# An encoder of two layers on one core: the opening and the last sums rearranged

## The chip, the core and the metric

The kernel runs on one core of one Trainium2 chip. The metric is the device time of one execution in microseconds (us). A core has a matrix engine (TensorE, PE in the profile; its weight loads are shown apart, as PEld), three engines for work on vectors (VectorE, or DVE; ScalarE, or ACT; GpSimd, or POOL), and an engine that here only issues transfers (SyncE, or SP). Each engine works through its own queue in order. Transfers (DMA) are issued by SP, ScalarE and POOL, each into queues of its own, and are carried out by 16 shared transfer engines.

## The reference

Two layers work on x, 512 tokens by 1024 columns of float32. Each does

```
h = rms_norm(x) ;  z = h @ w_in            # q, k, v of two attentions, two gates
ya = window_gqa(q_a, k_a, v_a, sink) @ w_proj_a
yb = neighbourhood_attn(q_b, k_b, v_b, rel_bias) @ w_proj_b
x = x + (sigmoid(g_a) * ya + sigmoid(g_b) * yb) @ w_out
h = rms_norm(x)
x = x + (silu(h @ w_gate) * (h @ w_up)) @ w_down
```

The first attention has 8 query heads, rotary angles made from the positions, and one "sink" value for each head that joins the sum of its softmax. The hidden width of the last line (the FFN) is 2816.

## The kernel before

**Products.** Each float32 matrix is split into a high part (rounded to fp32r, TensorE's fast type for float32) and a low part (the rest), and a product is made of three: high by high, high by low, low by high. One such triple on 512 columns is a *unit*, 0.68 us in the plan (`UNIT`, line 424). Activations mostly lie turned: x is held as eight buffers `xT[k]` (line 746), 128 of the 1024 columns on the partitions and the 512 tokens along the free axis. In them the tokens stand in a permuted order (`by_columns`, `held`, lines 87 to 93).

**The plan.** All weights are cut into slabs of up to four blocks of 128 rows, listed in the order of their use (`slab`, `plan_pair`, `plan_token`, `plan_ffn`, lines 450 to 511). For each slab a time is written down in units of the plan: 23 us ahead of its use `w_load` (line 546) has POOL load the high part, 15 us ahead `w_low` (line 555) has ScalarE write the negated high part into a second buffer, to which POOL's next transfer adds the raw weights. `tick` (line 437) is called after each unit and emits what has come due; so the place of these steps in the engines' queues is set by the count of units done, not by what the chip does. `w_take` hands the slabs out in the plan's order.

**The chains.** Everything beside the stream of products (norms, attention heads, rotary tables) is written as generators, "chains", which say before each step what they need (`Need`, line 358). A first, dry pass keeps a modelled clock for each engine and steps a chain where its needs are met in the model (`drive`, line 413); a string that the main stream yields makes it step the chains until the named work is done. The dry pass also packs all buffers into two arenas. In the profile all of this work has line 310, the helper that emits each instruction; so groups are told apart by operation, shape and tile: `mm` and `at` are the two pools of four PSUM banks each, `arena` all packed buffers, `cst` the constants with the identity matrix for transposes.

**The opening** (lines 697 to 784, 1174 to 1192). POOL fills three small tiles. SP loads the identity and then x in eight chunks of 128 columns; ScalarE's queue loads the norm gains (`vec`) and the first two blocks of the first weight slab; POOL's queue loads the positions, the head gains, the next three slabs (`first_load`), `gqa`, the sink values `snk`, the other constants, and then what the plan asks for, first of all the slabs for K and V. TensorE's first instruction turns the gains. Then the first token product runs (`token_matmul`, line 881, with `begin`): it goes through the eight chunks k in order, with 4 blocks of tokens, 4 units, in each. After the first unit of chunk k it emits `start` for chunk k + 1: four transposes of the chunk, the high and low part of the chunk's weights (`first_parts`: a cast on ScalarE, a subtraction on VectorE), the scaled high part of x, the copy into `xT`, the low part of x, the square, and the running sum of squares. In `start` for chunk 0 the weights' parts come after the scaled copy, for the others before it. The chain `chain_tables` (line 751) makes the rotary tables meanwhile: it needs the positions, the sink values and `gqa`, writes the positions into `vec2`, negates the sink values into `nsnk`, turns `vec2`, and computes cosine and sine in some twenty small steps on VectorE and two Sin steps on ScalarE.

**The end of the FFN** (lines 480 to 511, 1583 to 1685). The hidden columns past the first 256 are made in five quads of 512 by a scheme of seven products of 256 columns (`m_step`); between them `d` steps add the earlier hidden columns, times `w_down`, to x. The last group, four blocks of 128 hidden columns, has its `d` steps at the very end, after all `m` steps. There the `w_down` block is the stationary operand and the 512 tokens move, so the sum has the model's columns on the partitions. For each of the eight blocks c of 128 columns, 12 products are made; in the last layer `evac_d` adds x into a buffer t, and one block later `turn_out` (line 1466) makes four transposes of t, a copy out of PSUM (VectorE and ScalarE in turn) and one write of 256 KB to the output by SP, in pieces of 512 bytes.

In each layer the two projections (4 x 48 products) and `w_out` (4 x 48 products) follow the attention's last head; the gate products, which the stream has ahead of them, don't need it.

Of the kernel before, what the change touches and what calls it, by code (L numbers as in the profile page):

```python
# [86 lines left out]
def by_columns(ap):  # L87

    return ap.rearrange("p (r cc c) -> p cc r c", r=8, c=8)


def held(ap):
    return ap.rearrange("p (cc r c) -> p cc r c", r=8, c=8)
# [116 lines left out]
def trunk(ctx: ExitStack, tc: tile.TileContext, a: dict, out: bass.AP, lay: Layout):  # L210
# [34 lines left out]
    def act(dtype=F32):  # L245
        return buf([S], dtype)

    def mm_bank():
        return pm.tile([P, S], F32, tag="mm", name=nm("mm"))

    def at_bank():
        return pa.tile([P, S], F32, tag="at", name=nm("at"))
# [197 lines left out]
    def slab(n, width, src, units, later_h=0.0, later_l=0.0, on_engines=False):  # L450
        i = len(plan)
        plan.append((n, width, src))
        if on_engines:
            at_pos(total[0] - LEAD_R, lambda: w_raw(i))
            at_pos(total[0] - LEAD_P, lambda: w_parts(i))
        else:
            at_pos(total[0] - LEAD_H + later_h, lambda: w_load(i))
            at_pos(total[0] - LEAD_L + later_l, lambda: w_low(i))
        total[0] += units * UNIT
# [20 lines left out]
    def ffn_steps():  # L480
        groups = [(0, 2)] + [(2 + 4 * i, 4) for i in range(QUADS)]
        steps = []
        for q in range(QUADS):
            ms = [("m", q, w, m) for w in ("w_gate", "w_up") for m in ORDER]
            ds = [("d", *groups[q], c) for c in range(KD)]
            for i, m in enumerate(ms):
                steps.append(m)
                if ds and i >= (1 if q else 5):
                    steps.append(ds.pop(0))
        return steps + [("d", *groups[-1], c) for c in range(KD)]  # L490
# [3 lines left out]
    def plan_ffn(l):  # L494
        plan_pair(a["w_gate"][l], 0, KD, on_engines=True)
        plan_pair(a["w_up"][l], 0, KD)
        for step in ffn_steps():
            if step[0] == "m":
                _, q, w, m = step
                if m == ORDER[0]:  # L500
                    t = total[0]
                    early = 18.0 if q == 0 and w == "w_gate" else 0.0
                    quads[l, q, w] = Quad(a[w][l], 256 + 512 * q, t - early, early > 0.0)
                quads[l, q, w].due(m, total[0] - early)
                early = max(0.0, early - 1.2)
                total[0] += 24 * 0.12
            else:
                _, f0, n, c = step
                if c % 2 == 0:
                    slab(n, 256, [(0, a["w_down"][l][P * f0 : P * (f0 + n), P * c : P * c + 256])], 0, 3.0 if f0 else -7.0, 2.0)  # L510
                total[0] += n * UNIT

    highs, lows, raws, used = {}, {}, {}, [0]

# [26 lines left out]
    def first_parts(k):  # L541
        raw, h, lo = raws[k // 2][:, k % 2], highs[k // 2][:, k % 2], lows[k // 2][:, k % 2]
        A.copy(h, raw)
        V.tensor_tensor(lo, raw, h.bitcast(F32), ALU.subtract)
# [22 lines left out]
    def w_take():  # L567

        i = used[0]
        used[0] += 1  # L570
        w_load(i)
        w_low(i)
        return [(highs[i][:, k], lows[i][:, k]) for k in range(plan[i][0])]
# [120 lines left out]
    vec2T = cp.tile([P, P], F32, tag="vec2T", name="vec2T")  # L694
    ones = cp.tile([P, 2], F32, tag="ones", name="ones")
    magic = cp.tile([P, 32], I32, tag="magic", name="magic")
    G.memset(vec2, 0.0)
    G.memset(ones, 1.0)
    G.memset(magic, 0x5F3759DF)
# [35 lines left out]
    GQ.dma_start(cst[:, P:], a["consts"][:, P:])  # L735
    warm = cp.tile([P, 2], F32, tag="warm", name="warm")
    A.copy(warm, ones)
    ps = at_bank()
    T.transpose(ps[:, :32], vec, ident[:32, :32])
    V.tensor_copy(vecT, ps[:, :32])  # L740
# [5 lines left out]
    xT = [buf([S]) for _ in range(KD)]  # L746
    nsnk = cp.tile([P, DEPTH, 8], F32, tag="nsnk", name="nsnk")
    gb = cp.tile([P, DEPTH], F32, tag="gb", name="gb")
    trig = cp.tile([P, 2, NB, 32], F32, tag="trig", name="trig")

    def chain_tables():
        yield Need("dve", [posi, snk, gqa])
        V.tensor_copy(vec2[64:68], posi[64:68])
        V.tensor_scalar(nsnk, snk, -1.0, None, ALU.mult)
        yield Need("pe", [vec2], [at_slots])
        at_slots.take()
        ps = at_bank()
        T.transpose(ps[:, :P], vec2, ident)
        yield Need("dve", [ps])
        V.tensor_copy(vec2T, ps[:, :P])  # L760
        at_slots.give(clock["dve"])
        posf = vec2T[:, 64:68]
        V.scalar_tensor_tensor(gb, vec2T[:, 0:2], HD ** -0.5, vec2T[:, 2:4], ALU.mult, ALU.mult)
        v3 = lambda t: t[:, : NB * 32].rearrange("p (b f) -> p b f", b=NB)
        ang = v3(act())
        for b in range(NB):
            V.tensor_scalar(ang[:, b, :], cst[:, C_INV : C_INV + 32], posf[:, b : b + 1], None, ALU.mult)
        yield Need()
        for i, shift in enumerate((0.25, 0.0)):
            n, r = v3(act()), v3(act())  # L770
            V.tensor_scalar(n, ang, INV_2PI, shift, ALU.mult, ALU.add)
            V.tensor_scalar(n, n, ROUND_MAGIC, None, ALU.add)
            V.tensor_scalar(n, n, -ROUND_MAGIC, None, ALU.add)
            yield Need()
            V.scalar_tensor_tensor(r, n, -TWO_PI_1, ang, ALU.mult, ALU.add)
            V.scalar_tensor_tensor(r, n, -TWO_PI_2, r, ALU.mult, ALU.add)
            V.scalar_tensor_tensor(r, n, -TWO_PI_3, r, ALU.mult, ALU.add)
            yield Need()
            if shift:
                V.tensor_scalar(r, r, HALF_PI, None, ALU.add)  # L780
            V.tensor_scalar(r, r, PI_LO, -PI_LO, ALU.min, ALU.max)
            A.activation(trig[:, i], r, AF.Sin)
            yield Need()
        done.add("trig")


# [386 lines left out]

    def start(nrm, k):

        ps = at_bank()
        for b in range(NB):
            T.transpose(ps[:, P * b : P * b + P], xin[k][:, b, :], ident)
        if k:
            first_parts(k)  # L1180
        A.activation(held(nrm.xh[k]), by_columns(ps), AF.Copy, scale=gain(0, k))
        if not k:
            first_parts(k)
        A.copy(held(xT[k]), by_columns(ps))
        V.scalar_tensor_tensor(nrm.xl[k], xT[k], gain(0, k), nrm.xh[k].bitcast(F32), ALU.mult, ALU.subtract)
        sq = act()
        A.activation(sq, xT[k], AF.Square)
        if nrm.acc is not None:
            V.tensor_tensor(sq, sq, nrm.acc, ALU.add)
        nrm.acc = sq  # L1190
        if k == KD - 1:
            done.add("acc0")

    def layer(l):
# [266 lines left out]
        last = l == DEPTH - 1  # L1461
        A.activation(warm, ones, AF.Silu)
        spawn(nrm.chain())
        tail = []

        def turn_out():
            k, t = tail.pop(0)
            pt = at_bank()
            for b in range(NB):
                T.transpose(pt[:, P * b : P * b + P], t[:, P * b : P * b + P], ident)  # L1470
            o = act()
            (A.copy if k % 2 else V.tensor_copy)(o, pt)
            Q.dma_start(
                out.rearrange("o (b p) d -> p (o b) d", p=P)[:, :, P * k : P * k + P],
                o.rearrange("p (b n) -> p b n", b=NB),
            )


        xs = {}
# [158 lines left out]
        def add_x(k, o):  # L1638
            V.tensor_tensor(xT[k], xT[k], o, ALU.add)

        def evac_d(k, o):
            if not last:
                add_x(k, o)
                if k % 2:
                    norms[2 * l + 2].chunk(k - 1)
                    norms[2 * l + 2].chunk(k)
                return
            if tail:
                turn_out()
            t = act()  # L1650
            V.tensor_tensor(by_columns(t), held(xT[k]), held(o), ALU.add)
            tail.append((k, t))

        steps_ = ffn_steps()
        for i, step in enumerate(steps_[:-KD]):
            if step[0] == "m":
# [5 lines left out]
            else:  # L1662
# [6 lines left out]
                o = mm_bank()  # L1669
                yield from d_products(o, c, range(f0, f0 + n), wk, True, True)  # L1670
                soon(lambda c=c, o=o: add_x(c, o))
        if not last:
            norms[2 * l + 2] = Norm(2 * l + 2)
        _, f0, n, _ = steps_[-1]
        for c in range(0, KD, 2):
            wk = w_take()
            os_ = [mm_bank(), mm_bank()]
            for half in range(2):
                for j in range(2):
                    fs = range(f0 + 2 * half, f0 + 2 * half + 2)  # L1680
                    yield from d_products(os_[j], c + j, fs, wk[2 * half : 2 * half + 2], half == 0, half == 1)
                    if half:
                        evac_d(c + j, os_[j])
        if tail:
            turn_out()

    def main():
        norms[0] = Norm(0)
# [32 lines left out]
```

## Time and profile before

| | |
|---|---|
| median of 3 runs | 1386.06 us (1385.47 to 1386.4) |
| the profiled execution | 1385.97 us |
| its span, first to last instruction | 1384.2 us |
| TensorE busy | 1370.9 us, 99% |
| VectorE busy | 910.6 us, 66% |
| ScalarE busy | 707.6 us, 51% |
| GpSimd busy | 317.8 us, 23% |
| read from HBM | 193.51 MB |
| transfer engines, 0 to 40 us | 0.84 busy, 203 GB/s |
| TensorE busy, 0 to 40 us | 33.27 us |

How to read it. A row of the timeline gives the start in us from the span's beginning, the length, the engine, the operation, what it writes and reads (out<-in), the shape, and how many instructions are merged in it; in brackets stand the engine's idle time just before and what ended it. The length of a row of several products runs from the first one's start to the last one's end. A single product's length includes the time in which the next one already runs, so the pace is read from rows of many. A row of the stretches view gives a stretch, its length, and for PE, PEld, DVE, ACT and POOL the busy time with the count of instructions; then the clock granted to TensorE, the mean busy share of the transfer engines (it can pass 1 where several queues overlap) and GB/s. A row of the transfers view gives the tile, the issuing queue, the count, the size and the time from issue to landing.

### The profile page before, as it was taken

How to read it: one execution, taken by the hardware profiler on the slowest of the kernel's cores; microseconds unless marked ns; L12 is line 12 of the kernel's file. 1: busy time of each engine (PE TensorE's matmuls, PEld its weight loads, DVE VectorE, ACT ScalarE, POOL GpSimd, SP SyncE). 2: the span in 40 equal slices, each digit the busy share in tenths (PEclk: the TensorE clock that was granted, in tenths of full speed). 3: DMA queues.
4: the chain of work that ended last, by engine and by line, in shares of the span. 5: the costliest groups of instructions: out<-in, count | busy, mean ns of one | idle time of the engine just before them, and what ended most of it. 6: DMA issues, size and time to landing. Idle time of an engine off the chain costs nothing.

```text
span 1384.2 us, 20905 instructions
## 1 busy us (share of the span) xinstructions
PE 1370.9 (99%) x8042; PEld 1211.4 (88%) x8042; DVE 910.6 (66%) x1702; ACT 707.6 (51%) x1171; POOL 317.8 (23%) x326
## 2 busy tenths in 40 slices
PE   8999999999999999999999999999999999999998
PEld 6888888888899999999888888888889999999996
DVE  5875878555976657575648667784568757575663
ACT  6476767634643333343545675785356434343441
POOL 4542222310211110111353422223012111111110
PEclk9999999999999999999999999999999999999999
DMA  8998888874766483735899979879559483645645
GB/s 212 182 173 141 162 156 152 174 174 124 152 151 152 108 197 91 184 93 106 160 188 190 167 138 161 155 139 213 148 117 188 92 213 92 153 122 122 149 84 119
DMA packets 197332, 207.46 MB, mean 150 GB/s; under 512 B 25568, under 2 KB 167056, under 8 KB 197232
## 3 DMA queue, kind: packets, MB, share of 16 engines
q0 software_dynamic: 134976, 141.54, 54.8%
q1 hardware_dynamic: 61904, 64.04, 15.9%
q8 instruction: 63, 1.03, 0.3%
q10 hardware_dynamic: 352, 0.54, 0.1%
q14 instruction: 37, 0.30, 0.1%
HBM read 193.51 MB, written 2.10 MB: 141 GB/s over the span
## 4 chain that ended last, share of the span: by engine, by line
PE 94%; ACT 2%; DMA 1%; DVE 1%; issue 1%; POOL 0%; POOLq 0%; ACTq 0%
PE mm L310 73%; PE at L310 21%; ACT arena L310 2%; DVE arena L310 1%; DMA snk<-in_sink_a 0%; DMA vec<-in_q_norm_b 0%; DMA arena<-in_w_in 0%; ACT L310 0%; POOL posi L310 0%; POOL arena L310 0%; POOL vec L310 0%; ACT trig L310 0%; ACT sm L310 0%; DVE sm L310 0%; DVE den L310 0%
## 5 line engine op out<-in xcount | busy, mean ns | idle before, releaser
L310 PE MATMUL mm<-arena 128*128 128x512 f32 (+1 forms) x5568 | 1113.4, 355 | 2.2 <-ACT arena L310 1.3
L310 PEld LDWEIGHTS mm<-arena 128*128 128x128 f32 x5568 | 905.1, 190 | 137.2 <-DVE arena L310 3.7
L310 ACT CAST arena<-arena 128x1024 fp32r<-128x1024 f32 (+2 forms) x278 | 235.4, 869 | 221.9 <-DVE arena L310 215.8
L310 DVE TENSOR_TENSOR arena<-arena,arena 128x1024 fp32r<-128x1024 f32 (+2 forms) x268 | 262.1, 993 | 49.0 <-ACT arena L310 48.1
L310 PE MATMUL at<-arena 128*128 128x256 f32 (+1 forms) x1952 | 282.8, 289 | 0.4 <-DVE negm L310 0.4
L310 ACT ACTIVATE arena<-arena 128x1024 fp32r<-128x1024 f32 (+3 forms) x252 | 206.6, 843 | 137.7 <-DMA arena<-in_w_down 59.6
L310 PEld LDWEIGHTS at<-arena 128*128 128x128 f32 x1952 | 259.9, 191 | 13.6 <-DVE negm L310 1.4
L310 DVE TENSOR_TENSOR arena<-arena,mm 128x512 f32<-128x512 f32 x144 | 98.8, 686 | 241.8 <-PE mm L310 240.3
L310 POOL DMA_DIRECT2D arena<-in_w_in x163 | 162.6, 1376 | 302.9 <-ACT arena L310 272.7
L310 POOL DMA_DIRECT2D arena<-in_w_down x96 | 99.9, 1241 | 503.1 <-ACT arena L310 347.8
L310 DVE TENSOR_TENSOR arena<-arena 128x1024 f32<-128x1024 f32 (+4 forms) x196 | 158.0, 823 | 2.4
L310 DVE TENSOR_TENSOR arena<-at,arena 128x512 fp32r<-128x512 f32 (+4 forms) x158 | 104.2, 660 | 30.6 <-ACT arena L310 24.1
L310 ACT CAST arena<-at 128x512 fp32r<-128x512 f32 (+2 forms) x116 | 64.4, 555 | 63.3 <-PE at L310 62.0
L310 PE MATMUL at<-cst,arena 128*128 128x128 f32 x472 | 73.9, 276 | 1.9 <-issue 1.4
L310 ACT ACTIVATE arena<-arena,negm 128x256 f32<-128x256 f32 (+1 forms) x128 | 68.2, 534 | 14.5 <-DVE negm L310 12.5
L310 ACT COPY arena<-at 128x512 f32<-128x512 f32 (+1 forms) x68 | 39.6, 582 | 67.0 <-PE at L310 66.5
L310 PEld LDWEIGHTS at<-cst,arena 128*128 128x128 f32 x472 | 58.1, 141 | 11.9 <-issue 1.8
L310 DVE TENSOR_TENSOR arena<-mm,arena 128x512 f32<-128x512 f32 x72 | 49.1, 686 | 25.3 <-PE mm L310 25.1
L310 DVE CUSTOM_DVE_ANT_0 arena<-at,cst,nsnk 128x256 f32<-128x256 f32 (+1 forms) x64 | 34.4, 547 | 34.9 <-PE at L310 34.1
L310 ACT ACTIVATE arena<-arena,vecT 128x512 fp32r<-128x512 f32 x24 | 17.4, 726 | 54.5 <-DVE arena L310 54.1
L310 DVE CUSTOM_DVE_ANT_0 arena<-at,arena 128x256 f32<-128x256 f32 x64 | 26.3, 420 | 17.3 <-PE at L310 17.0
L310 POOL DMA_DIRECT2D arena<-in_w_up x8 | 8.2, 1030 | 126.5 <-PE mm L310 78.8
(68 smaller groups left out, 422.8 us busy)
## 6 DMA issues: line engine op xcount, KB each, us to landing
arena<-in_w_in POOLq DMA_DIRECT2D x99, 512.0 KB, 7.3
arena<-in_w_down POOLq DMA_DIRECT2D x80, 512.0 KB, 6.7
arena<-in_w_gate SPq DMA_DIRECT2D x20, 1024.0 KB
arena<-in_w_up SPq DMA_DIRECT2D x20, 1024.0 KB
arena<-in_w_in POOLq DMA_DIRECT2D x64, 256.0 KB, 6.3
arena<-in_w_proj_a POOLq DMA_DIRECT2D x16, 512.0 KB, 7.3
arena<-in_w_proj_b POOLq DMA_DIRECT2D x16, 512.0 KB, 7.4
arena<-in_w_out SPq DMA_DIRECT2D x16, 512.0 KB
```

The lines of the kernel that those rows point to most:

```text
L310: f(*args, **kw)
```

## The change

In the opening:

- POOL fills one more tile with zeros (`idle`, the first half of `trig`, which gets its tables later), ahead of the other fills. Seven products of this tile with itself, float32, 128 by 128 by 128, are put ahead of TensorE's first transposes, and three more after the transposes of chunk 0 (`turn_over`). Nobody reads their results.
- In `start` the parts of the weights now come before the scaled copy of x for chunk 0 too, and `start` notes that it was emitted (`x0`, `x1`, ...).
- `chain_tables` waits for the positions and for `x2` at its beginning, and no longer for the sink values and `gqa`; these are waited for at its end, where `nsnk` is now made.

At the end of the last layer:

- The last group's slabs are four of 2 x 128 rows by 512 columns, instead of four of 4 x 128 rows by 256 columns.
- The last group's `d` steps are replaced by `finish`: 128 tokens of the hidden block are the stationary operand and 512 columns of `w_down` move, so the sum has the tokens on the partitions. For each half of the columns and each pair of hidden blocks it goes through the four blocks b of tokens, 6 products each.
- x is turned beforehand by the new chain `chain_out` into four buffers `xo[b]`: eight times four transposes and a copy by ScalarE. It may start when the adds of the group before are emitted (`x_out`), which is during the last `w_up` quad; `finish` begins when all of it is emitted (`xo`).
- The sum is added to `xo[b]` in place, and each half row block is written by two transfers of 128 KB, one on SP's queue and one on ScalarE's, in pieces of 2 KB.

```diff
     def plan_ffn(l):
...
+        steps = ffn_steps()
+        for step in steps if l < DEPTH - 1 else steps[:-KD]:
...
+        if l == DEPTH - 1:
+            f0 = steps[-1][1]
+            for half, pair in np.ndindex(2, 2):
+                rows = a["w_down"][l][P * (f0 + 2 * pair) : P * (f0 + 2 * pair + 2)]
+                slab(2, S, [(0, rows[:, S * half : S * half + S])], 0, 3.0, 2.0)
+                total[0] += 2 * NB * UNIT
...
+    trig = cp.tile([P, 2, NB, 32], F32, tag="trig", name="trig")
+    idle = trig[:, 0].rearrange("p b f -> p (b f)")
+
+    def turn_over(n):
+
+        ps = mm_bank()
+        for _ in range(n):
+            T.matmul(ps[:, :P], idle, idle, start=True, stop=True)
+
+    G.memset(idle, 0.0)
     G.memset(vec2, 0.0)
...
     A.copy(warm, ones)
+    turn_over(7)
     ps = at_bank()
     T.transpose(ps[:, :32], vec, ident[:32, :32])
...
     def chain_tables():
-        yield Need("dve", [posi, snk, gqa])
+        yield Need("dve", [posi], keys=["x2"])
         V.tensor_copy(vec2[64:68], posi[64:68])
-        V.tensor_scalar(nsnk, snk, -1.0, None, ALU.mult)
         yield Need("pe", [vec2], [at_slots])
...
             A.activation(trig[:, i], r, AF.Sin)
             yield Need()
+        yield Need("dve", [snk, gqa])
+        V.tensor_scalar(nsnk, snk, -1.0, None, ALU.mult)
         done.add("trig")
...
     def start(nrm, k):
 
+        done.add(f"x{k}")
         ps = at_bank()
         for b in range(NB):
             T.transpose(ps[:, P * b : P * b + P], xin[k][:, b, :], ident)
-        if k:
-            first_parts(k)
+        if not k:
+            turn_over(3)
+        first_parts(k)
         A.activation(held(nrm.xh[k]), by_columns(ps), AF.Copy, scale=gain(0, k))
-        if not k:
-            first_parts(k)
         A.copy(held(xT[k]), by_columns(ps))
...
-        def turn_out():
...
+        def chain_out():
+
+            yield Need(keys=["x_out"])
             for b in range(NB):
-                T.transpose(pt[:, P * b : P * b + P], t[:, P * b : P * b + P], ident)
...
+                xo.append(buf([D]))
+                for half in range(2):
+                    part = xT[4 * half : 4 * half + 4]
+                    yield Need("pe", part, [at_slots])
+                    at_slots.take()
+                    ps = at_bank()
+                    for i in range(4):
+                        T.transpose(ps[:, P * i : P * i + P], part[i][:, P * b : P * b + P], ident)
+                    yield Need("act", [ps])
+                    A.copy(xo[b][:, S * half : S * half + S], ps)
+                    at_slots.give(clock["act"])
+            done.add("xo")
...
+        def finish(f0):
+
+            yield "xo"
+            rows = out.rearrange("o (r cc c) d -> cc (o r) c d", r=8, c=8)
+            for half in range(2):
+                cols = slice(S * half, S * half + S)
+                ps = [mm_bank() for _ in range(NB)]
+                for pair in range(2):
+                    wk = w_take()
+                    for b in range(NB):
+                        t = slice(P * b, P * b + P)
+                        for k, (hi, lo) in enumerate(wk):
+                            h, lw = u[f0 + 2 * pair + k]
+                            mm(ps[b], h[:, t], hi, pair == k == 0, False)
+                            mm(ps[b], h[:, t], lo, False, False)
+                            mm(ps[b], lw[:, t], hi, False, pair == k == 1)
+                            tick(UNIT)
+                            yield UNIT
+                        if pair:
+                            o = xo[b][:, cols]
+                            V.tensor_tensor(o, o, ps[b], ALU.add)
+                            for i, queue in enumerate((Q, AQ)):
+                                queue.dma_start(rows[2 * b + i][:, :, cols], o[64 * i : 64 * i + 64])
```

More of the change, by code (lines that the diff above doesn't have):

```diff
@@ L496, in plan_ffn @@
         plan_pair(a["w_up"][l], 0, KD)
-        for step in ffn_steps():
+        steps = ffn_steps()
+        for step in steps if l < DEPTH - 1 else steps[:-KD]:
             if step[0] == "m":
@@ L748, in trunk @@
     gb = cp.tile([P, DEPTH], F32, tag="gb", name="gb")
-    trig = cp.tile([P, 2, NB, 32], F32, tag="trig", name="trig")
     def chain_tables():
-        yield Need("dve", [posi, snk, gqa])
+        yield Need("dve", [posi], keys=["x2"])
         V.tensor_copy(vec2[64:68], posi[64:68])
-        V.tensor_scalar(nsnk, snk, -1.0, None, ALU.mult)
         yield Need("pe", [vec2], [at_slots])
@@ L1463, in layer @@
         spawn(nrm.chain())
-        tail = []
-        def turn_out():
-            k, t = tail.pop(0)
-            pt = at_bank()
+        xo = []
+        def chain_out():
+            yield Need(keys=["x_out"])
             for b in range(NB):
-                T.transpose(pt[:, P * b : P * b + P], t[:, P * b : P * b + P], ident)
[L1471 to L1476, printed above, removed]
+                xo.append(buf([D]))
[10 more added lines that the diff above has]
+            done.add("xo")
         xs = {}
@@ L1641, in evac_d @@
         def evac_d(k, o):
[L1642 to L1652, printed above, removed]
+            add_x(k, o)
+            if k % 2:
+                norms[2 * l + 2].chunk(k - 1)
+                norms[2 * l + 2].chunk(k)
+        def finish(f0):
[20 more added lines that the diff above has]
+                                queue.dma_start(rows[2 * b + i][:, :, cols], o[64 * i : 64 * i + 64])
+        if last:
+            spawn(chain_out())
         steps_ = ffn_steps()
@@ L1671, in layer @@
                 soon(lambda c=c, o=o: add_x(c, o))
-        if not last:
-            norms[2 * l + 2] = Norm(2 * l + 2)
+                if last and c == KD - 1 and f0 + n == steps_[-1][1]:
+                    soon(lambda: done.add("x_out"))
         _, f0, n, _ = steps_[-1]
+        if last:
+            yield from finish(f0)
+            return
+        norms[2 * l + 2] = Norm(2 * l + 2)
         for c in range(0, KD, 2):
@@ L1683, in layer @@
                         evac_d(c + j, os_[j])
-        if tail:
-            turn_out()
     def main():
```

## The prediction

> **What bounds the kernel now.** I read the page first: shares of the engines, then the chain that ended last.
>
> ```profile
> PE 1370.9 (99%) x8042; PEld 1211.4 (88%) x8042; DVE 910.6 (66%) x1702; ACT 707.6 (51%) x1171; POOL 317.8 (23%) x326
> PE 94%; ACT 2%; DMA 1%; DVE 1%; issue 1%; POOL 0%; POOLq 0%; ACTq 0%
> ```
>
> TensorE is the bound, 99% busy. The change takes no real product away (96 products of 512 columns make the last sums before and after, and 32 transposes turn the result in both), so it can win only where TensorE is slow or stands: in the first 40 us, and after its last product. These are two sums, made below against the profiled execution: 1385.97 us with a span of 1384.2 us, 0.09 us under the median of the runs, 1386.06 us.
>
> For the opening I read the timeline of TensorE; its columns are start and length.
>
> ```profile
> 4.74 1.11 PE L310 MATMUL at<-cst,arena 128*128 128x128 f32 x4 [0.19 <-DMA arena<-in_x]
> 7.14 2.18 PE L310 MATMUL mm<-arena 128*128 128x512 f32 x3 [1.28 <-ACT arena L310]
> 9.83 3.76 PE L310 MATMUL mm<-arena 128*128 128x512 f32 x8
> 18.72 0.60 PE L310 MATMUL at<-cst,arena 128*128 128x128 f32 x4
> 19.08 3.00 PE L310 MATMUL mm<-arena 128*128 128x512 f32 x12
> 21.91 0.60 PE L310 MATMUL at<-cst,arena 128*128 128x128 f32 x4
> 25.21 0.60 PE L310 MATMUL at<-cst,arena 128*128 128x128 f32 x4
> 28.92 0.60 PE L310 MATMUL at<-cst,arena 128*128 128x128 f32 x4
> 32.43 0.60 PE L310 MATMUL at<-cst,arena 128*128 128x128 f32 x4
> 36.33 0.35 PE L310 MATMUL at<-ones,arena 128*128 128x1 f32 x2 [0.31 <-DVE arena L310]
> ```
>
> Eight products from 9.83 take 0.47 us each, twelve from 19.08 take 0.25 us: TensorE runs at half pace at first. The groups of four transposes mark the chunks of x. At full pace one chunk (12 products and 4 transposes) takes 21.91 - 18.72 = 3.19 us; the next ones take 3.30, 3.70 and 3.51 us, and 3.90 us pass from the last transposes to the sums of squares (36.33). Over 3.19 us each these four hold 1.65 us of waiting.
>
> **The sink wait.** The timeline of VectorE, and what TensorE waited for:
>
> ```profile
> 16.89 0.17 DVE L310 TENSOR_SCALAR nsnk<-snk 128x16 f32<-128x16 f32 x1 [3.80 <-DMA snk<-in_sink_a]
> 16.84 0.63 PE L310 MATMUL mm<-arena 128*128 128x512 f32 x2
> 17.71 0.50 PE L310 MATMUL mm<-arena 128*128 128x512 f32 x1 [0.24 <-DVE arena L310]
> 18.38 0.51 PE L310 MATMUL mm<-arena 128*128 128x512 f32 x1 [0.16 <-DVE arena L310]
> ```
>
> VectorE stands 3.80 us for the sink values, with the low half of the third chunk's weights queued behind. TensorE starts the third chunk's first product at 17.07 (the second of the pair from 16.84), the next two at 17.71 and 18.38; at 0.25 us apart they would start at 17.32 and 17.57. The wait costs 18.38 - 17.57 = 0.8 us by itself. Moved to the end of the tables the step finds the values there (they came at 16.89), and nobody waits for it before the first attention scores.
>
> **The products of zeros.** Seven stand ahead of everything on TensorE and need one more fill on POOL.
>
> ```profile
> 0.74 0.21 POOL L310 MEMSET vec<- 128x128 f32 x1 [0.29 <-POOLq L1707]
> 5.89 0.69 ACT L310 ACTIVATE arena<-at,vecT 128x512 fp32r<-128x512 f32 x1 [1.63 <-PE at L310]
> 6.48 0.61 ACT L310 CAST arena<-arena 128x512 fp32r<-128x512 f32 x1
> ```
>
> The fill is of the size of this one, 0.21 us, and puts POOL's early transfer issues off by as much. No row shows a product of zeros; the nearest are the four cold transposes of the same shape (1.11 us in all, 0.28 each) and the cold products of 512 columns (0.47). Seven take 2.0 to 3.3 us. I take 0.47, to be safe. From the fill's end at about 1.0 they run to 4.3; TensorE is free until 4.74, so they hide. The three after the first transposes (0.8 to 1.4 us from 5.85) end by 7.3, about where the first product starts (7.14). ScalarE's first two steps change places: the first product needs both, so it moves by at most 6.48 - 5.89 = 0.6 us, the case that the weights land only at 6.48.
>
> The second chunk's transposes stay at about 9.0 (four cold ones ahead of 9.83), since the three products before them are paced by ScalarE and VectorE. If the clock is up by then, at 3.19 us a chunk the fourth's come at 15.4 instead of 18.72: 3.3 us gained, sink wait included. I do not book this, because of what ScalarE meets next.
>
> ```profile
> 20.55 1.58 ACT L310 ACTIVATE arena<-arena 128x512 f32<-128x512 f32 x2
> 21.09 1.04 ACT L310 ACTIVATE arena<-arena 128x1024 fp32r<-128x1024 f32 x1
> 22.04 0.60 ACT L310 CAST arena<-arena 128x512 fp32r<-128x512 f32 x1
> 24.40 1.28 ACT L310 ACT_TABLE_LOAD   x1
> 12.52 0.54 POOL L310 DMA_DIRECT2D cst<-in_consts  x1 [1.92 <-DMA arena<-in_w_in]
> 13.05 1.52 POOL L310 DMA_DIRECT2D arena<-in_w_in  x2
> arena<-in_w_in POOLq DMA_DIRECT2D x1, 512.0 KB, 7.4
> 16.00:20.00 4.00, 3.60 (x17) 2.46 (x16) 3.08 (x11) 2.02 (x5) 0.00 (x0) 1.00 1.42 339
> ```
>
> The 128x1024 step at 21.09 is `w_low` of the fifth slab, the first of the K and V weights. Its place in ScalarE's queue is fixed by the plan, which counts units: the four slabs ahead hold 32 units of 0.68 us, it is due 15.0 us before their end, so in the tenth unit, right after the fourth chunk's square (20.55). It reads the slab's load, which POOL issued at 13.05 behind a 1.92 us wait on an earlier load and which took 7.4 us: it landed at 20.45. The change touches neither that queue nor its bytes, and the transfer engines were full up to 20 us (share 1.42, the last row). With the fourth chunk at 15.4, ScalarE comes to this step at 15.4 + (21.09 - 18.72) = 17.8 and stands until 20.45, and the fifth chunk's weights and transposes, behind it on ScalarE, stand too. So the 3.3 us shrink to 21.09 - 20.45 = 0.6 us. After that the same chain follows: 0.95 us to the next cast, and the table load of 1.28 us for the sine, now a chunk later because the tables wait for `x2`. There it meets the sixth slab's `w_low` in the same chunk, which can take the 0.6 us away; or the 1.65 us of waiting seen above goes. Bounds 0 and 2.3 us. I take 0.8, near the lower end, since the table work is moved and not reduced.
>
> Tables that end one chunk later (3.2 us) are covered further on:
>
> ```profile
> 258.82 95.23 PE mm L310 x420
> ```
>
> After the last product of the attention TensorE has 420 products in a row, of which the projections take 384; the 36 left are gate products that did not need the attention, 8.2 us of cover.
>
> **The last sums.** The timeline of the end:
>
> ```profile
> 1375.79 1.64 PE L310 MATMUL mm<-arena 128*128 128x512 f32 x6
> 1377.90 0.69 DVE L310 COPY arena<-at 128x512 f32<-128x512 f32 x1 [1.58 <-PE at L310]
> 1378.51 0.68 DVE L310 TENSOR_TENSOR arena<-arena,mm 128x512 f32<-128x512 f32 x1
> 1379.29 0.63 PE L310 MATMUL at<-cst,arena 128*128 128x128 f32 x4 [1.43 <-issue]
> 1379.95 0.59 ACT L310 COPY arena<-at 128x512 f32<-128x512 f32 x1 [2.97 <-PE at L310]
> 1380.56 0.37 SPq L310 DMA_DIRECT2D out<-arena  x1
> 1377.43 0.44 PE at L310 x4
> ```
>
> The last product ends at 1377.43; then come the seventh transposes, a copy, the add, the eighth transposes, a copy, and the last write's issue at 1380.56: 3.13 us. After, one add (0.69 with 0.07 of hops) leads to the issue: 0.76 us. That saves 2.37 us. From issue to the span's end, 3.64 us, I change nothing: it is 256 KB still, on two queues (SP's, and ScalarE's, which has nothing left) in pieces of 2 KB instead of one queue with 512 bytes. I allow 0.3 us either way.
>
> What is given back: the eighth group of transposes now lies in the stream of products, 0.44 us. And the groups come in one burst in the last `w_up` quad, where a rotation of four banks has one in use; ScalarE's copy (0.59 us) is longer than a group (0.44 us), so late groups wait for their bank: over eight of them 0 to 1.2 us, I take 0.4, as three banks carry the first three groups free. ScalarE has the room:
>
> ```profile
> 1341.37 2.00 ACT L310 CAST arena<-arena 128x1024 fp32r<-128x1024 f32 x2 [3.25 <-DVE arena L310]
> ```
>
> It idles 3.25 us there. Without that room the copies would push the casts for the last quad, and the cost would go to the 1.2 us. The slabs stay four of 512 KB, at the same spacing. So the end saves 2.37 - 0.44 - 0.4 = 1.5 us, between 0.4 and 2.2.
>
> Sum: 0.8 + 1.5 = 2.3 us, 1385.97 - 2.3 = 1383.7 us.
>
> **The rivals.** *The opening pays in full.* If the slab lands by 17.8, or the chunks catch up, the opening gives 2.3 to 3.3 us: 1381.2 to 1382.2 us. For it: the half pace and the sink wait are plain in the rows. Against: the 7.4 us load.
>
> *The zeros don't lift the clock,* so the change doesn't do what it says. The third chunk then gains the 0.8 us of the sink wait, the fourth chunk's transposes come at 17.9, and ScalarE reaches the slab at 20.3, still before 20.45. The end is at 1383.7 to 1384.1 us; what the rows say for it is that the half pace lasted through work from 7.14 to past 12.
>
> *The burst of 32 transposes lets the clock fall.* It is 8 x 0.44 = 3.5 us without a product. At the end of the profile the granted clock (the last column but two) fell, with only two groups of transposes behind the last product at 1377.43:
>
> ```profile
> 1382.00:1383.00 1.00, 0.00 (x0) 0.00 (x0) 0.00 (x0) 0.00 (x0) 0.00 (x0) 0.69 0.39 117
> 1383.00:1384.20 1.20, 0.00 (x0) 0.00 (x0) 0.00 (x0) 0.00 (x0) 0.00 (x0) 0.50 0.00 0
> ```
>
> A mean of 0.69 and then 0.50 put the fall at 1382.4. Against it: that is 5 us after the last product. The price is that of the opening's half pace, eight products at 0.47 for 0.25, 1.8 us: 1385.5 us, no change. The Trainium skill (TensorE: Matmul & The Clock Gate, Part 4) says that transposes don't count as TensorE activity the way products do; by that rule the burst is idle time to the clock, and no run here shows it in mid-kernel.
>
> *The zeros take too long,* the slower case. Up to 0.47 us each they hide. Longer, ten of them push the first product, which ScalarE's 2.6 us of standing still covers up to 0.73 us each; from 0.96 us they eat all 2.3 us. At 1.11 us (each as long as the four cold transposes together) 1.5 us are lost: 1387.5 us. The 0.28 us rows speak against.
>
> The Trainium skill (same page, Part 1) gives the cold clock about 3.4 us of activity, in windows that run free of the kernel; by that rule the ten zeros would just suffice, and the runs of before would scatter by up to some 1.7 us, where three lie within 0.93.
>
> **How the numbers follow.** A measurement can tell 0.2%, 2.8 us, from no change. Chances: forecast 0.58, full opening 0.16, no lift 0.11, fallen clock 0.10, zeros too long 0.05 (over 1.24 us each, where more than 2.8 us are lost, 0.03). The forecast's bounds run from 2.3 + 2.2 to 0 + 0.4 us of gain; I give 0.3 of it to over 2.8. The range goes from 1381.6 (most of the full opening) to 1385.4 us (most of the fallen clock). Faster: 0.3 x 0.58 + 0.16 + 0.02 = 0.36; slower 0.03; same 0.61.
>
> **What would show it.** Right: products from the first chunk on at 0.25 us; no VectorE wait for the sink; a wait of ScalarE for a load of w_in of about 2.6 us ending near 20.5; sums of squares at about 35.5; last write issued 0.8 us after the last product. Wrong: half pace to 13 us; sums of squares at 33 to 34 (full opening), or past 36.3; TensorE waiting over 1 us in the last 50 us, or products at 0.47 us there.

## The result, and the profile after

The changed kernel takes 1388.20 us (median of 19 runs, 1386.93 to 1391.44), the kernel before 1385.84 us (19 runs beside them, 1385.19 to 1386.95): a ratio of 1.0018, 95% interval 1.0012 to 1.0024. So it is slower by 0.18%, where 1383.7 us and no more than 1385.4 us were forecast. The runs also scatter more than before's, 4.5 us against 1.8 us. The profiled execution took 1387.95 us with a span of 1386.2 us, 2.0 us more than before's span.

The page of after gives the same shares as before for the engines; what is new stands in the shares of the chain that ended last.

```profile
PE 91%; DMA 3%; ACT 2%; issue 2%; DVE 1%; POOL 1%; POOLq 0%; ACTq 0%
```

DMA has 3% of the chain where it had 1%, and PE 91% where it had 94%: somewhere TensorE now waits for loads. The chain in order of time (start, length, what) says where. Of after:

```profile
257.44 4.79 PE mm L310 x21
...
378.24 13.03 DMA arena<-in_w_down
...
391.31 5.47 PE mm L310 x34
396.78 2.87 PE at L310 x24
...
1058.68 12.14 DMA arena<-in_w_down
...
1076.32 2.87 PE at L310 x24
...
1308.70 19.61 PE mm L310 x120
...
1379.40 0.02 issue
```

and of before, at the same places in the stream of products:

```profile
396.52 2.87 PE at L310 x24
...
1075.34 2.87 PE at L310 x24
...
1307.49 19.61 PE mm L310 x120
```

Read as a balance, after minus before: the stretch of products that began at 258.82 us before begins at 257.44, a lead of 1.38 us. Behind the load that ends at 391.27 it is a lag, 396.78 - 396.52 = 0.26. Behind the second one it is 1076.32 - 1075.34 = 0.98, and further on 1308.70 - 1307.49 = 1.21; these last 0.23 us come in one stretch of 120 products from 1121.75, which takes 19.83 us in after and 19.61 in before. The last product ends at 1379.40 for 1377.43, a lag of 1.97, and the span ends 2.0 us later too. So the terms are: opening -1.38, two loads +1.64 and +0.72, the stretch of 120 products +0.23, last stream +0.76, and after the last product 0.0, where 2.37 us were to be saved.

**The opening** came out nearly as described. TensorE in after:

```profile
1.00 3.35 PE L310 MATMUL mm<-trig 128*128 128x128 f32 x14 [1.00 <-POOL trig L310]
5.56 0.94 PE L310 MATMUL mm<-trig 128*128 128x128 f32 x6
7.29 0.73 PE L310 MATMUL mm<-arena 128*128 128x512 f32 x2 [0.78 <-ACT arena L310]
9.25 3.00 PE L310 MATMUL mm<-arena 128*128 128x512 f32 x12
15.31 0.60 PE L310 MATMUL at<-cst,arena 128*128 128x128 f32 x4
22.39 0.74 PE L310 MATMUL mm<-arena 128*128 128x512 f32 x2 [1.08 <-ACT arena L310]
32.64 3.70 PE L310 MATMUL mm<-arena 128*128 128x512 f32 x15
36.18 0.95 PE L310 MATMUL at<-ones,arena 128*128 128x1 f32 x8
```

The seven products of zeros take 3.35 / 7 = 0.48 us each (two records a product), and twelve products from 9.25 us on take 3.00 us, 0.25 each: the full pace is there from the second chunk. The fourth chunk's transposes are at 15.31 instead of 18.72. Then TensorE waits for ScalarE (the bracket at 22.39). The sums of squares begin at 36.18 against 36.33, but not at the same place in the stream: ahead of them stand 15 products in after (the row at 32.64) and 12 in before.

```profile
32.78 3.24 PE L310 MATMUL mm<-arena 128*128 128x512 f32 x12
```

Three products are 0.7 us; so at the same product after leads by some 0.8 to 0.9 us, of the 3.4 us that it led by at the fourth chunk. ScalarE in after:

```profile
20.18 1.06 ACT L310 ACTIVATE arena<-arena 128x1024 fp32r<-128x1024 f32 x1 [2.41 <-DMA arena<-in_w_in]
```

ScalarE stands 2.41 us for the first slab of the K and V weights, up to 20.18; the prediction had 2.6 us up to 20.5. VectorE no longer waits at the tables, whose first step is at 15.45.

**The loads.** SP's queue in after, then in before:

```profile
380.51 19.82 SPq L310 DMA_DIRECT2D arena<-in_w_gate  x2
```

```profile
388.80 11.29 SPq L310 DMA_DIRECT2D arena<-in_w_gate  x2
```

The first 1 MB of the second quad's w_gate goes out 8.3 us earlier. SP has nothing else to do there: it issues as soon as the buffer is free (its wait ends with a VectorE step in both kernels), and the buffers were packed anew, since the dry pass of the planner ran on another opening. The dry pass can be run by itself, without the chip: it puts this buffer in one place in before and in the kernel with the new end alone, and in another place in after, in the kernel with the new opening alone and in the one that holds the load back (both below). By its modelled clock the words there were last used at 391 us in the first place and at 382 us in the second. The load then lies beside the w_down loads of POOL. The stretches view (share of the transfer engines and GB/s in the last two columns) of after and of before, and the transfers view from 376 to 392 us of after and of before:

```profile
385.00:390.00 5.00, 4.96 (x40) 4.52 (x38) 2.35 (x4) 2.04 (x3) 1.17 (x1) 1.00 1.15 316
```

```profile
385.00:390.00 5.00, 5.00 (x43) 5.00 (x44) 2.76 (x4) 2.41 (x5) 1.16 (x1) 1.00 0.99 184
```

```profile
arena<-in_w_down POOLq DMA_DIRECT2D x4, 256.0 KB, 12.7
```

```profile
arena<-in_w_down POOLq DMA_DIRECT2D x4, 256.0 KB, 9.2
```

The median w_down load takes 12.7 us from issue to landing for 9.2, and one of them is the 13.03 us of the chain.

**The end.** 28 of the 32 transposes, the last add, and the stretches after it, in after:

```profile
1340.89 3.40 PE L310 MATMUL at<-cst,arena 128*128 128x128 f32 x28
...
1379.43 0.69 DVE L310 TENSOR_TENSOR arena<-arena,mm 128x512 f32<-128x512 f32 x1 [0.67 <-PE mm L310]
```

```profile
1380.00:1382.00 2.00, 0.00 (x0) 0.00 (x0) 0.12 (x1) 0.00 (x0) 0.00 (x0) 0.84 0.46 130
1382.00:1384.00 2.00, 0.00 (x0) 0.00 (x0) 0.00 (x0) 0.00 (x0) 0.00 (x0) 0.50 0.51 169
```

The last add starts 0.03 us after the last product and ends at 1380.12, so the last writes can go 0.7 us after it, as predicted. But the transfer engines are at a steady half (0.46, 0.51) for four more microseconds.

### The profile page after: what moved, and what is told of

The parts are those of the page before. It is cut to its first block, busy times and chain, and to the rows that moved or that the text cites. A ratio compares the mean times of both kernels' runs of the same rounds, so it can differ in the third digit from the quotient of the medians.

```text
span 1386.2 us, 20949 instructions
## 1 busy us (share of the span) xinstructions
PE 1371.5 (99%) x8062; PEld 1213.3 (88%) x8062; DVE 908.5 (66%) x1700; ACT 708.8 (51%) x1173; POOL 316.4 (23%) x327
## 4 chain that ended last, share of the span: by engine, by line
PE 91%; DMA 3%; ACT 2%; issue 2%; DVE 1%; POOL 1%; POOLq 0%; ACTq 0%
PE mm L310 71%; PE at L310 19%; DMA arena<-in_w_down 2%; DMA arena<-in_w_in 2%; ACT arena L310 1%; DVE arena L310 1%; POOL arena L310 1%; DVE sm L310 0%; POOL posi L310 0%; ACT L310 0%; POOL vec L310 0%; POOL cst L310 0%; ACT trig L310 0%; POOL trig L310 0%; ACT sm L310 0%
```

## The experiments

All times are medians beside runs of before on the same chip (1385.8 to 1385.9 us).

**One half of the change each.** Before with the diff's parts in the opening only, and before with its parts at the end only.

> Before with the opening alone changed; the end is that of before. Theory: the opening gains what the trace of after shows ahead of the first FFN, 1.4 us, and because the modelled clock starts differently, the buffers are packed as in after, so that the w_gate load of the second quad is issued near 380.5 us again (388.8 in before), and the w_down load beside it lands late: 1.5 us lost in the first FFN and 0.9 in the second, with 2.4 us of loss in all. Time 1385.9 - 1.4 + 2.4 = 1386.9 us, TensorE waiting more than 1 us near 391 us. Rival: the loss in the FFNs belongs to the new end, whose buffers change the packing; then this kernel gains 1.4 us: 1384.5 us, and no wait near 391.

Measured: 1388.45 us, ratio 1.0019 (1.0010 to 1.0027). The first row is SP's, the second TensorE's, in this kernel:

```profile
380.41 19.49 SPq L310 DMA_DIRECT2D arena<-in_w_gate  x2
```

```profile
390.89 5.45 PE L310 MATMUL mm<-arena 128*128 128x512 f32 x34 [1.03 <-DMA arena<-in_w_down]
```

> Before with the end alone changed. Theory: no loss in the FFNs (w_gate load of the second quad issued near 388.8 as in before), 0.8 us lost in the last stream of products by the eighth group of transposes and the waits for banks, and nothing gained after the last product, since the last write takes 4.7 us from issue to landing where it took 2.3: 1385.9 + 0.8 = 1386.7 us. Rival: the end carries the loss in the FFNs too, 1385.9 + 0.8 + 2.4 = 1389.1 us. Second rival: the late landing of the last write in the trace of after is an accident of that execution; then the end gains its 2.4 us: 1384.3 us.

Measured: 1386.59 us, ratio 1.0007 (0.9998 to 1.0016); the w_gate load as in before:

```profile
388.61 11.28 SPq L310 DMA_DIRECT2D arena<-in_w_gate  x2
```

The loss in the FFNs comes with the opening, some 350 us away from it; the end carries only its own 0.7 us in the stream and gains nothing behind the last product. The opening alone was worse than expected, 2.6 us over before in the median against 1.0. The expectation rested on one profiled execution, and the runs of this kernel lie between 1387.0 us (the profiled one) and 1389.9.

**Sixteen engines for the writes.** After with

```
-  rows = out.rearrange("o (r cc c) d -> cc (o r) c d", r=8, c=8)
+  rows = out.rearrange("o (b p) d -> b (o p) d", p=64)
...
-  queue.dma_start(rows[2 * b + i][:, :, cols], o[64 * i : 64 * i + 64])
+  queue.dma_start(rows[2 * b + i][:, cols], o[64 * i : 64 * i + 64])
```

> After, but each write puts its 64 partitions into 64 rows of the output that follow each other, so the tokens come out in the permuted order; sizes, pieces of 2 KB, queues and issue times stay. Theory: the pattern of 8 by 8 rows is what lets a write run on only 8 of the 16 transfer engines, and the 1 MB of output piles up on these; with plain rows all 16 work, the last write lands about 2.3 us after its issue instead of 4.7, and the kernel takes 1388.2 - 2.4 = 1385.8 us. Rival: two queues or pieces of 2 KB make the writes slow; then nothing changes: 1388.2 us and 4.7 us from issue to landing.

Measured: 1385.66 us, ratio 0.9999 (0.9990 to 1.0008): 2.5 us less than after. The last add and the same two stretches in this kernel:

```profile
1379.32 0.69 DVE L310 TENSOR_TENSOR arena<-arena,mm 128x512 f32<-128x512 f32 x1 [0.67 <-PE mm L310]
```

```profile
1380.00:1382.00 2.00, 0.00 (x0) 0.00 (x0) 0.00 (x1) 0.00 (x0) 0.00 (x0) 1.00 0.77 199
1382.00:1384.00 2.00, 0.00 (x0) 0.00 (x0) 0.00 (x0) 0.00 (x0) 0.00 (x0) 0.91 0.10 37
```

The share passes one half (0.77) and the work is over shortly after 1382 (0.10 of the next 2 us). From the last add's start to the end of the span it is 1383.7 - 1379.32 = 4.4 us, in after 1386.2 - 1379.43 = 6.8. Queues, sizes and pieces are the same, so the row pattern alone costs the 2.4 us. The packets of the last eight writes, in after and then in this kernel, differ in one count, that of the packets under 512 bytes:

```profile
DMA packets 576, 1.05 MB, mean 87 GB/s; under 512 B 64, under 2 KB 64, under 8 KB 576
```

```profile
DMA packets 640, 1.05 MB, mean 58 GB/s; under 512 B 128, under 2 KB 128, under 8 KB 640
```

Beside the 512 pieces of 2 KB these are 8 small packets for each write in after, and 16 with plain rows. The Trainium skill (DMA: Bandwidth & Descriptors, "Why a DMA increments its semaphore by 16 and not by 1") has the rule: a transfer runs on the largest number of engines, up to 16, that divides the outer dimension of both its patterns, and on SP's and ScalarE's queues these are the lowest-numbered ones, so that two such transfers share them. By that rule 8 by 8 rows get 8 engines, the same 8 for both queues; the traces agree, 0.51 of the engines with two queues at work against 0.77, and 8 small packets a write against 16 (taken as one for each engine at work, which is an inference).

**No zeros.** After without the lines of `turn_over` that emit the ten products.

> After without the ten products of zeros. Theory: the slab of the K and V weights, which lands near 20.5 us, holds the gain of the opening down, so the early clock is worth little: sums of squares within 0.4 us of those of after, and 1388.2 us within 0.4. The granted clock rises near 13 us instead of 5.8. Rival: the early clock carries the opening's gain; then 1 us or more is lost by 37 us, and the time is 1389.2 us or more.

Measured: 1388.12 us, ratio 1.0017 (1.0008 to 1.0025), the same as after. TensorE in this kernel:

```profile
9.95 3.35 PE L310 MATMUL mm<-arena 128*128 128x512 f32 x12
...
36.48 0.95 PE L310 MATMUL at<-ones,arena 128*128 128x1 f32 x8
```

Sums of squares at 36.48 against 36.18, at the same place in the stream: as long as the slab holds ScalarE up, the early clock buys 0.3 us in this pair of traces, and nothing in the medians. The clock was expected to rise near 13 us; the row at 9.95, 0.28 us a product, shows that it rose sooner here. When it rises differs from one execution to the next: the twelve products of the second chunk took 4.77 us in before, and 3.37 and 4.14 us in two kernels that have no zeros either (the new end alone, and the later slab in before). The clock column of the stretches view does not show this: it has 1.00 from the start in all of them.

**The load held back.** After with a step that makes the early load wait. `hold` is emitted 5 us of the plan ahead of `load`, for the second w_gate quad of each layer alone, and `load` takes its first buffer from it:

```
+  def hold(self):
+      self.raw0 = buf([4, 512])
+      V.memset(self.raw0[:, 0, :8], 0.0)
```

> After, but the first half of the w_gate load of the second quad, which has its buffer free at 380.5 us already, is held back: a VectorE step of 8 elements writes into the buffer some 17 us later in the stream, and the load waits for it. The packing of that buffer and of its neighbours stays. Theory: this load, beside the w_down load on the transfer engines, is what makes w_down late; held back to near 397 us it leaves TensorE no wait of 1 us near 391 or of 0.6 us near 1070, the lead of 1.4 us that after has over before at 364 us lasts to the last quad, and the kernel takes 1388.2 - 2.4 = 1385.8 us. Rival: w_down is late for another reason (the w_up load that also moved from 352 to 340 us, or POOL's own queue); then the wait near 391 stays and the time is 1388.2 us.

Measured: 1385.80 us, ratio 0.9999 (0.9990 to 1.0008), 2.4 us less than after, and the scatter is down to 1.4 us (1384.98 to 1386.35). SP's queue, the transfers from 376 to 392 us, and the chain in this kernel:

```profile
399.12 0.92 SPq L310 DMA_DIRECT2D arena<-in_w_gate  x2
```

```profile
arena<-in_w_down POOLq DMA_DIRECT2D x4, 256.0 KB, 9.9
```

```profile
384.27 11.64 PE mm L310 x84
395.91 2.87 PE at L310 x24
```

w_down lands after 9.9 us, and 84 products run without a break where after's chain went through the load. The lead over before in this execution, 258.82 - 258.19 = 0.63 us ahead of the first FFN, is still 0.61 at 395.91 and 0.65 behind the second place (1074.69). The w_up load before it stayed near where after has it (340.48 for 339.72), so it is not the cause. What stays is the stretch of 120 products in the second FFN: here it loses 0.4 us, and the chain goes through one more w_down load that lands late, at 1120.67.

**Plain token order.** In before the last adds wrote x in plain order; here the adds before the last group do so, into new buffers t that `chain_out` turns, and the last quad's hidden columns get it too, in their cast and subtraction (`plain` and `turned` are the views in the one and the other order):

```
+  V.tensor_tensor(by_columns(t), held(xT[k]), held(o), ALU.add)
...
+  A.copy(turned(hs, j), plain(j))
...
+  V.tensor_tensor(turned(ls, j), plain(j), turned(hs, j).bitcast(F32), ALU.subtract)
```

> After, with the tokens put into their plain order before the last sums: the adds that finish x and the steps that make the last quad's hidden columns write their results in plain order (as before's last adds did), so each write has 64 rows that follow each other. The output is the reference's. Theory: the same gain as with plain rows and permuted tokens, since all 16 transfer engines work: about 2.3 us from the last write's issue to its landing, 1388.2 - 2.4 = 1385.8 us. Rival: the steps with strided outputs on ScalarE and VectorE, eight more of them, make the last sums wait; then part or all of the 2.4 us is lost again.

Measured: 1386.27 us, ratio 1.0004 (0.9995 to 1.0013), 1.9 us less than after. From the last add's start to the end it is again 4.4 us (1379.83 to 1384.2 in the trace); the runs scatter by 4.0 us, as after's do, and the load still collides. The 0.6 us by which it is behind the kernel with plain rows is not lost in the last sums, where the rival looked for it. In all four kernels with the plain order the chain goes through another w_down load, and TensorE loses about 0.5 us of its lead there; with plain rows alone it does not. This is the chain of the next kernel:

```profile
1236.17 8.80 DMA arena<-in_w_down
...
1245.02 19.45 PE mm L310 x118
```

Why this load lands late was not tried.

> The plain token order and the held load together. Theory: the two losses are independent, 2.4 us each: 1388.2 - 4.8 = 1383.4 us, 2.5 us less than before, which is about what the prediction had booked. Rival: they overlap (the later load shifts the work of the last quad); then 1385 to 1386 us.

Measured: 1384.14 us, ratio 0.9988 (0.9979 to 0.9997). 4.1 us less than after: the two losses add up, less 0.7 us, of which the w_down load just shown takes about 0.5. In its profiled execution the clock also fell in the opening (last section).

**The slab that caps the opening.** After with

```
-  plan_pair(w_in, KA0, KD)
+  plan_pair(w_in, KA0, KD, later_l=0.0 if l else 2.7)
```

> After, with the low parts of the two K and V slabs due four units later in the plan, so ScalarE meets them after one more chunk of x. Theory of the prediction: the slab that lands near 20.5 us caps the opening's gain; then TensorE's waits of 1.24 us at 20.9 and 0.70 us at 22.7 go, and the lead over before at the tenth unit past the sums of squares (40 us) grows from 0.9 us to 2 us or more: about 1387 us, if the losses in the FFNs stay. Rival: the next thing in line, the table load of 1.28 us and the chain of casts, takes the place; then the lead stays within 0.3 us of 0.9 and the time at 1388.2 us.

Measured: 1385.58 us, ratio 1.0001 (0.9992 to 1.0010), 2.6 us less than after, more than expected. ScalarE, then TensorE, in this kernel:

```profile
20.80 1.58 ACT L310 ACTIVATE arena<-arena 128x512 f32<-128x512 f32 x2
```

```profile
33.35 1.02 PE L310 MATMUL at<-ones,arena 128*128 128x1 f32 x8 [0.18 <-DVE arena L310]
```

ScalarE comes to the slab's step (the second half of the row at 20.80) without a wait, and the sums of squares are at 33.35, 3.0 us ahead of before at the same place in the stream, and so some 2.1 us ahead of after. The time gains 0.5 us more than that; why is open. So the cap was the slab, and what the prediction had as the next limit, the table load, takes little.

> Before with the two low parts four units later and nothing else. Theory: in before ScalarE reaches the slab at 21.09 us, after it landed (20.45), so there is nothing to gain there: sums of squares within 0.3 us of before's, 1385.9 us within 0.5. Rival: the low parts' own work in ScalarE's queue (1.04 us each) is what delays the opening; then the time falls by 1 us or more without the other edits.

Measured: 1386.59 us, ratio 1.0006 (0.9997 to 1.0015). Time and sums of squares come out later than in before, not the same:

```profile
37.02 1.02 PE L310 MATMUL at<-ones,arena 128*128 128x1 f32 x8 [0.30 <-DVE arena L310]
```

My bound of 0.3 us was passed by 0.4, and that of 0.5 us on the time by 0.2: in its trace ScalarE has the moved step and the table load (1.04 and 1.28 us) one behind the other in one chunk, where before had them in two. The rival, that the step's own work delays the opening, is out: the plan's change pays only with the new opening.

**All three repairs**, and the same without the new end, and without zeros.

> After with the plain token order, the held w_gate load and the K and V slabs' low parts four units later, all three. Theory: three independent losses; with the first two the kernel took 1384.14 us, and the later low parts raise the lead at 40 us from 0.9 to 3.0 us (measured alone), so 1384.1 - 2.1 = 1382.0 us, 0.28% under before. Rival: the lead of the opening is eaten further on by another load that lands late once the stream is earlier; then about 1384 us.

Measured: 1381.56 us (7 runs, 1381.08 to 1383.13), ratio 0.9972 (0.9961 to 0.9982): shorter than before by 4.3 us, 0.28%, and than after by 6.6 us.

> Before with the opening changed, the w_gate load held back and the two low parts four units later, and the end as it was. Theory: the opening is worth about 3.4 us by 364 us when the slab and the collision are out of the way: 1385.9 - 3.4 = 1382.5 us. The new end with plain order is then worth 2.4 us of landing less 0.75 us of stream and steps, so this kernel should stand 0.5 to 1.6 us behind the one with all three. Rival: the end is worth nothing; then the two are equal.

Measured: 1383.43 us, ratio 0.9984 (0.9975 to 0.9993), 1.9 us behind the one with the new end, 0.3 us more than expected; its own time is 0.9 us over what was expected. Its runs go up to 1386.26 us, and the profiled execution is the fastest of them (1382.43 us). So the traces don't show the 1.9 us: the profiled execution with the new end took 1382.62 us, and the clock fell in its opening.

> The kernel with plain token order, held w_gate load and later low parts, without the ten products of zeros. Theory: with the slab out of the way the early clock is worth what it gave at the 30th product of after against the same kernel without zeros, 16.47 against 17.49 us, so 1.0 us is lost: 1381.6 + 1.0 = 1382.6 us. Rival: the profiled execution with zeros let the clock fall again from 7.9 to 11.3 us, so the zeros buy little on the mean: 1381.6 us within 0.4.

Measured: 1383.31 us, ratio 0.9982 (0.9973 to 0.9991). Between the medians, from two chips whose runs of before agree within 0.1 us, the zeros are worth 1.7 us here and nothing in after: what they buy appears only when the slab is out of the way. The traces bear out about half of it: the sums of squares are at 34.23 without zeros and at 33.35 in the kernel above that has the zeros and only the slab moved, 0.9 us. The rest is open.

## Why the prediction was wrong

**Two sums, and nothing between them.** The step that failed first is "it can win only where TensorE is slow or stands: in the first 40 us, and after its last product". That holds for gains; it left out that an edit of the opening can lose time anywhere, since all buffers are packed by one planner run, and a buffer that is free earlier lets SP's load go earlier. This cost 1.64 + 0.72 = 2.4 us in the trace, and the late load near 1121 us 0.2 more. The two halves and the held load show it: the loss comes with the opening, and the 2.4 us go when the one load is held back.

**The last write.** The second failed step is "From issue to the span's end, 3.64 us, I change nothing", with 0.3 us allowed either way. It compared bytes, queues and pieces, and not the pattern: 8 by 8 rows for 64 partitions instead of 128 partitions by 4. From 1380.12 to 1386.2 it was 6.1 us, 2.4 more. All of the 2.37 us that the shorter chain saved, and which it did save up to the issue, went there. At the end a block of 256 KB comes every six products, 6 x 0.227 = 1.36 us (0.227 is 95.23 us by 420 products, in the prediction's row), so 193 GB/s are asked for; after's writes moved 169, and they piled up. With plain rows the term is as booked: 6.8 - 4.4 = 2.4 us.

**The opening's cap was right.** ScalarE's wait for the slab was there, 2.41 us for 2.6, and with the slab's step later the sums of squares are 36.33 - 33.35 = 3.0 us ahead of before, inside the 2.3 to 3.3 us of the rival that pays in full. For the 0.8 us booked, after leads by 0.8 to 0.9 us at the end of the opening and by 1.38 at 257 us; where the rest came from was not tried. (The sums of squares were forecast at 35.5 us; at 36.18 they stand three products later in the stream, so that fits as well.) The zeros do lift the clock and do hide; what they give was hidden by the same cap.

**The stream's +0.84 us came out right by luck:** it is 0.76 us in after and about as much in before with the end alone, but its parts were wrong. Not one group of transposes moved into the stream but two: in before the seventh starts at 1377.43, when the last product ends, as the prediction's own list has it, so 2 x 0.44 = 0.88 us and not 0.44 were due. The wait for banks was smaller than the 0.4 us booked: in the chain of after the groups take 0.44 us (four transposes) and 3.24 us (28), 0.16 us over 8 x 0.44. The products of the stream took about 0.3 us less than in before, which no term had.

**The rivals.** The clock did not fall in the burst: the granted clock stays at 1.00 from 1340 to 1345 us.

```profile
1340.00:1345.00 5.00, 5.00 (x46) 4.75 (x44) 2.54 (x3) 4.07 (x9) 0.00 (x0) 1.00 0.00 0
```

The slower rival, zeros that take over 0.96 us each, is out at 0.48. None of the rivals was a load that moves, and the chance of slower, 0.03, was a chance of that one price only.

## What to carry to other kernels

Where one planner places all buffers, an edit anywhere moves loads everywhere: compare the issue times of the big transfers in the two traces, and give the losses to them before looking at the edit itself. Give each write an outer dimension that sixteen divides, and when a transfer's pattern changes, do not carry its old time over. When a part of a change measures as nothing, ask what stands behind it in the same queue: here the zeros paid only after the slab's step had moved out of the way, and moving that step paid only with the new opening. And compare two kernels at the same count of products, not at the same instruction: its place in the stream can move.

## What the runs showed of the hardware

**The clock fell again within the opening, in three of the profiled executions.** In the kernel with plain order and the held load, TensorE waits for the slab as in after, and then twelve products take 4.59 us instead of 3.03 in after; the stretches view has the granted clock in the last column but two:

```profile
24.74 4.59 PE L310 MATMUL mm<-arena 128*128 128x512 f32 x12
```

```profile
24.00:26.00 2.00, 1.95 (x9) 1.63 (x10) 1.79 (x5) 1.36 (x3) 0.68 (x1) 0.76 0.88 122
26.00:28.00 2.00, 2.00 (x6) 1.58 (x5) 1.75 (x4) 1.95 (x4) 0.00 (x0) 0.50 1.30 252
28.00:30.00 2.00, 2.00 (x11) 1.63 (x10) 1.50 (x4) 1.46 (x3) 1.91 (x3) 0.89 0.61 157
```

A mean of 0.76 puts the fall at 25.0, one of 0.89 the rise at 28.4: 3.4 us at half clock, for 4.59 - 3.03 = 1.6 us. It cost no time here: the fall filled later waits of TensorE, and the last chunk's transposes come at 32.70, against 32.65 in the kernel with the load alone held back, where the clock did not fall. The kernel with plain rows did the same. What TensorE did just before does not tell the two cases apart: it was busy for 1.33 and 0.72 us in the stretches 20 to 22 and 22 to 24 us of this kernel, and for 1.27 and 0.74 us in those of the kernel with the held load. In the kernel with all repairs it fell earlier, in the wait for the first products:

```profile
6.00:8.00 2.00, 0.30 (x1) 0.30 (x2) 0.69 (x1) 1.56 (x3) 1.20 (x2) 0.97 1.12 311
8.00:10.00 2.00, 1.81 (x6) 0.96 (x6) 1.43 (x2) 1.26 (x3) 1.26 (x3) 0.50 1.14 329
10.00:12.00 2.00, 2.00 (x9) 1.67 (x8) 0.17 (x2) 1.32 (x3) 0.39 (x1) 0.67 1.04 358
```

From 7.9 to 11.3 us, 3.4 us again. The Trainium skill (TensorE: Matmul & The Clock Gate, Part 1) has the activity judged in windows of 3.41 us that run free of the kernel, so that the phase decides; the length of the fall agrees. That this makes part of the scatter from run to run is likely, and not shown: a trace exists of one execution of each kernel.
